# Attention in a two-block network: the value products of both heads of a pair share one bank of the small pool

## The chip, the cores and the metric

The kernel is one program on one core of a Trainium2 chip. The metric is the device time of one execution in microseconds (us), the median of three runs. The engines are named as in the profile: PE is TensorE (matmuls, and PEld its weight loads), DVE is VectorE, ACT is ScalarE, POOL is GpSimd, SP issues most of the DMAs.

## The reference, cut to what matters

Two small transformer networks run one after the other on 256 tokens of width 1024, everything in float32. The first has two layers: layer 0 with sparse and sliding-window attention (8 + 8 heads), layer 1 with dilated attention (16 heads). The second has two layers ("mixers") with two attention branches of 8 heads each, called fox and mla, beside a recurrent branch. All attention has this form per head, with 256 queries and 256 keys and a causal mask of one kind or another:

```
s  = einsum('qd,kd->qk', q, k) * scale          # scores
s  = where(mask, s, -inf)
p  = exp(s - max(s))
o  = einsum('qk,kd->qd', p, v) / sum(p)         # value products
...
def mixer layer:                                # second network
    z = rmsnorm(x) @ w_in                       # q, k, v of both branches, gates, recurrence
    y_b = attention of mla (z) @ w_br_b
    y_c = attention of fox (z) @ w_br_c
    merged = sigmoid(gates) * (y_a, y_b, y_c), summed
    x = x + merged @ w_o
    x = x + feed-forward(x)
```

Head size is 64; in the kernel a key of a fox head has 66 numbers and one of an mla head 96.

## The kernel before

Tokens lie in two tiles of 128 rows. All weight matrices are streamed: SP loads a block (`raw_block`, L216), ACT rounds it to the high part `wh` (L236), DVE takes the low part `wl` (L237), and PE multiplies three times per block (`mm3`, L249 to L253). These are the "dense" products.

The helper `attend` (L349) computes the attention of a pair of heads, and it runs 36 times: 12 times in layer 0 (`nsa_pair`, `b_pair`), 8 times in layer 1 (`attention`), 8 times in each mixer (`branch`, L993: four fox pairs, then four mla pairs). The steps of a pair, each once per head:

- scores (L358 through the helper `mm`): PE writes the scores of the first 128 queries to columns 256 to 383 of a PSUM bank and those of the other 128 queries to columns 0 to 255;
- softmax (L366, L367): DVE adds the mask and takes the row's minimum of the negated sum into `m`, ACT takes the exponent; both work on tile `pr` in SBUF;
- transposes (L375): PE turns the three 128x128 blocks of `pr` back into the same PSUM bank;
- eviction to `pt`: DVE for the first head (L381), ACT for the second (L379), or DVE for both with a multiplier in layer 1 (L377);
- value products (L385 to L387, recorded under L358): three matmuls of 65 columns. Column 64 of `v` is one, so it yields the sum of the exponents. They go to columns 0 to 129 of the same bank that held scores and transposes;
- DVE takes the reciprocal of the sums (L404) and scales the products into the accumulator (L398 and its like).

PSUM has eight banks in three pools: `psd` 2 banks (dense products), `psb` 4 banks, `psm` 2 banks. Before, a pair takes two banks of `psb`, one per head, and holds them from the first score to the last read of its value products, so two pairs fit. `psm` serves other short uses; in the mixers these are the transposes of queries and keys (`heads_T`, L983: four transposes per head, L986 and L988, then one copy by ACT, L990).

No order is written out by hand. A list scheduler orders the instructions of each engine by their place in the program and by when their inputs, a free buffer and their engine would be there. Each tag of a pool has a fixed number of buffers (`BUFS`, `psd`, `psb`, `psm`); a tile whose tag has none free waits, and in both programs the tiles of `psm`, and those of `psb`, are first written in the order in which the program names them. On the chip each engine takes its instructions strictly in the order that the scheduler fixed.

Of the kernel before, what the change touches and what calls it, by code (L numbers as in the profile page):

```python
# [147 lines left out]
def model(ctx: ExitStack, tc: tile.TileContext, A, out, taps=None):  # L148
# [4 lines left out]
    wk = pool("wk")  # L153
    sm = pool("sm", 12)
    ps = pool("ps", 1, space=bass.MemoryType.PSUM)
    BUFS = {"wr": 5, "wh": 5, "wl": 5, "xt": 16, "rg": 14, "acc": 2, "w512": 5, "qkT": 4, "pr": 2, "pt": 2, "vv": 8, "fa": 4, "qk": 2, "junk": 1, "cm": 1, "w128": 4}

    def tmp(shape, tag, name, dt=F32):
        return wk.tile([P] + list(shape), dt, name=name, tag=tag, bufs=BUFS[tag])

# [5 lines left out]
    def psb():  # L166
        return ps.tile([P, 512], F32, name="psb", tag="psb", bufs=4)

    def psm():
        return ps.tile([P, 512], F32, name="psm", tag="psm", bufs=2)  # L170
# [7 lines left out]
    def queue_after(ins, earlier):  # L178

        info = mybir.DependencyInfo(mybir.DependencyClass.NoSync, mybir.DependencyReason.DATA)  # L180
        for e in earlier:
            tc.add_manual_dep(ins.ins, e.ins.name, info, reason="function table")
        return ins
# [165 lines left out]
    def attend(q, k, v, mask, ct=False, sink=None):  # L349
# [4 lines left out]
        pr, pt = tmp([2, 384], "pr", "pr"), tmp([2, 384], "pt", "pt")  # L354
        two = lambda x: x.rearrange("p (a t) -> p a t", a=2)

        bank = [psb(), psb()]
        mm = lambda o, l, r, a, b: nc.tensor.matmul(o, l, r, start=a, stop=b, skip_group_check=True)  # L358
# [14 lines left out]
        for j in range(2):  # L373
# [5 lines left out]
                nc.scalar.activation(pt[:, j], bank[j][:, :384], AF.Copy)  # L379
            else:  # L380
                nc.vector.tensor_copy(pt[:, j], bank[j][:, :384])  # L381
        pov = []
        for j in range(2):
            o = bank[j][:, :130].rearrange("p (q e) -> p q e", q=2)
            mm(o[:, 0], pt[:, j, 256:], v(0, j), True, True)  # L385
            for kt in range(2):
                mm(o[:, 1], pt[:, j, kt * P:(kt + 1) * P], v(kt, j), False, kt == 1)  # L387
            pov.append(o)
# [148 lines left out]
    first = [win_e.load(*win_e.by[0][0])]  # L537
# [14 lines left out]
    def layer0(nm, after):  # L552
# [55 lines left out]
        for t in range(2):  # L608
            o = psd()
# [7 lines left out]
            z, e = small(24, "gz"), small(24, "ge")  # L617
# [7 lines left out]
        for t in range(2):  # L625
            o = psb()
# [142 lines left out]
        def attend_cmp(vbd):  # L769

            p = psm()
# [5 lines left out]
            th = lambda x: x.rearrange("p (t h) -> p t h", t=2)  # L777
            bc = lambda x: th(x)[:, :, :, None].to_broadcast([P, 2, 8, 16])
            per_t = lambda n: con(n)[:, :, None].to_broadcast([P, 2, 8])
            s = tmp([256], "cm", "cs")  # L780
            nc.vector.tensor_tensor(c4(s), c4(p[:, :256]), con("cmpm").rearrange("p (t c) -> p t c", t=2)[:, :, None, :].to_broadcast([P, 2, 8, 16]), op=ALU.add)
            m, dn, rc = (small(16, n_) for n_ in ("cm", "cd", "crc"))
            nc.vector.tensor_reduce(th(m), c4(s), axis=AX.X, op=ALU.max)
# [571 lines left out]
```

## Time and profile before

| | |
|---|---|
| median of three runs | 1586.75 us (1581.74 to 1588.69) |
| the profiled execution: its time | 1581.74 us |
| the profiled execution: its span, first to last instruction | 1580.0 us |
| PE busy | 1557.5 us, 99% of the span |
| DVE busy / ACT busy | 982.3 us (62%) / 855.3 us (54%) |
| TensorE clock granted, mean | 0.998 |

Stages in the span: layer 0 attention lies from about 38 to 122 us, layer 1 attention from 343 to 440 us, the attention of the first mixer from 690 to 742 us and that of the second from 1155 to 1207 us. Between them are dense products.

A PE that is busy is not always at its peak, since a matmul's end is modelled: two matmuls in a row overlap. So what PE does is read here by the distance of starts (the chain of waits lists those), and what it lacks by the idle part of a window.

### The profile page before, as it was taken

The numbers are of one execution on the slowest core, as the hardware profiler recorded it, in microseconds if no ns is written. First come the engines' busy times: TensorE is split into PE (matmuls) and PEld (weight loads), VectorE is DVE, ScalarE is ACT, GpSimd is POOL, SyncE is SP. The second block draws the span as 40 slices with busy tenths as digits, with TensorE's granted clock in tenths as the row PEclk, the third lists the DMA queues.
The fourth block names the chain that finished last, engine by engine and source line by source line (L and its number), as shares of the span: only waits on it lengthen the run. The fifth ranks groups of instructions, "written<-read, shape, count | busy, mean of one in ns | idle before, by whom it ended". The sixth has DMA issues, their size and how long they took to land.

```text
span 1580.0 us, 21686 instructions
## 1 busy us (share of the span) xinstructions
PE 1557.5 (99%) x7870; PEld 1314.7 (83%) x7870; DVE 982.3 (62%) x1778; ACT 855.3 (54%) x1385; POOL 140.3 (9%) x226
## 2 busy tenths in 40 slices
PE   8999999999999999999999999999999999999997
PEld 7778888899888888899888888888898888888886
DVE  6685545577765455576677655456575777655556
ACT  6555444455454444676474654446685564644445
POOL 2000000011100000120033000000020023000001
PEclk9999999999999999999999999999999999999999
DMA  7424655544545565451657555554552656465661
GB/s 270 149 92 133 206 184 184 187 141 131 182 131 191 186 192 188 161 180 40 196 179 233 174 181 192 186 188 160 177 169 71 204 189 197 161 201 185 197 195 61
DMA packets 80587, 269.53 MB, mean 171 GB/s; under 512 B 11360, under 2 KB 12768, under 8 KB 80480
## 3 DMA queue, kind: packets, MB, share of 16 engines
q1 hardware_dynamic: 80048, 267.10, 52.7%
q8 instruction: 62, 1.02, 0.3%
q10 hardware_dynamic: 432, 1.05, 0.2%
q14 instruction: 45, 0.37, 0.1%
HBM read 267.06 MB, written 1.05 MB: 170 GB/s over the span
## 4 chain that ended last, share of the span: by engine, by line
PE 96%; DVE 2%; ACT 1%; DMA 1%; issue 0%; POOL 0%; POOLq 0%; SPq 0%; DVEq 0%; ACTq 0%
PE psb L250 13%; PE psb L252 13%; PE psb L251 13%; PE psd L252 12%; PE psd L250 12%; PE psd L251 12%; PE psb L358 5%; PE psm L250 3%; PE psm L251 3%; PE psm L252 3%; PE psb L375 1%; PE psb L497 1%; DVE wl L237 1%; PE psb L270 1%; PE psm L270 1%; DMA wr<-w_in_e 1%
## 5 line engine op out<-in xcount | busy, mean ns | idle before, releaser
L237 DVE TENSOR_TENSOR wl<-wr,wh 128x1024 fp32r<-128x1024 f32 (+2 forms) x504 | 598.1, 1198 | 423.0 <-ACT wh L236 410.5
L236 ACT ACTIVATE wh<-wr 128x1024 fp32r<-128x1024 f32 (+2 forms) x504 | 512.6, 1029 | 474.0 <-PE psb L252 208.5
L251 PE MATMUL psb<-wl,th 128*128 128x512 f32 x912 | 349.4, 391 | 0.0
L252 PE MATMUL psb<-wh,tl 128*128 128x512 f32 x912 | 349.2, 390 | 0.0
L250 PE MATMUL psb<-wh,th 128*128 128x512 f32 x912 | 346.5, 391 | 0.0
L252 PE MATMUL psd<-wh,tl 128*128 128x512 f32 (+4 forms) x696 | 255.7, 370 | 3.4 <-DVE tl L279 3.4
L250 PE MATMUL psd<-wh,th 128*128 128x512 f32 (+4 forms) x696 | 258.2, 375 | 0.0
L251 PE MATMUL psd<-wl,th 128*128 128x512 f32 (+4 forms) x696 | 255.0, 369 | 0.5 <-DVE wl L237 0.5
L252 PEld LDWEIGHTS psb<-wh,tl 128*128 128x128 f32 x912 | 171.2, 188 | 35.7
L250 PEld LDWEIGHTS psb<-wh,th 128*128 128x128 f32 x912 | 171.3, 188 | 35.3
L251 PEld LDWEIGHTS psb<-wl,th 128*128 128x128 f32 x912 | 171.3, 188 | 35.2
L252 PEld LDWEIGHTS psd<-wh,tl 128*128 128x128 f32 x696 | 131.2, 188 | 22.7 <-DVE tl L279 5.0
L251 PEld LDWEIGHTS psd<-wl,th 128*128 128x128 f32 x696 | 131.5, 189 | 17.5 <-DVE wl L237 0.9
L250 PEld LDWEIGHTS psd<-wh,th 128*128 128x128 f32 x696 | 131.3, 189 | 17.5 <-issue 1.7
L306 POOL TENSOR_SCALAR rest<-ss 128x1 f32<-128x1 f32 x24 | 7.2, 299 | 919.4 <-ACT junk L316 919.4
L367 ACT ACTIVATE pr<-pr,m 128x128 f32<-128x128 f32 (+1 forms) x144 | 58.3, 447 | 29.9 <-DVE m L366 28.1
L250 PE MATMUL psd<-wh,hth 128*128 128x512 f32 x176 | 71.9, 412 | 0.0
L251 PE MATMUL psd<-wl,hth 128*128 128x512 f32 x176 | 68.8, 391 | 0.0
L251 PE MATMUL psm<-wl,hth 128*128 128x512 f32 x176 | 68.5, 389 | 0.0
L250 PE MATMUL psm<-wh,hth 128*128 128x512 f32 x176 | 68.5, 389 | 0.0
L252 PE MATMUL psm<-wh,htl 128*128 128x512 f32 x176 | 67.8, 389 | 0.0
L487 ACT ACTIVATE sg<-psb,r 128x256 f32<-128x256 f32 x88 | 41.8, 475 | 48.0 <-PE psb L252 47.8
(320 smaller groups left out, 1759.9 us busy)
## 6 DMA issues: line engine op xcount, KB each, us to landing
wr<-w_gate_up SPq DMA_DIRECT2D x176, 512.0 KB, 4.3
wr<-w_down SPq DMA_DIRECT2D x88, 512.0 KB, 3.3
wr<-w_in SPq DMA_DIRECT2D x88, 512.0 KB, 4.0
wr<-w_qkv_o SPq DMA_DIRECT2D x32, 384.0 KB, 3.5
wr<-w_o SPq DMA_DIRECT2D x16, 512.0 KB, 4.1
wr<-w_ple_gate SPq DMA_DIRECT2D x16, 512.0 KB, 4.0
wr<-w_in_e SPq DMA_DIRECT2D x10, 512.0 KB, 4.7
wr<-w_out_e SPq DMA_DIRECT2D x8, 512.0 KB, 4.6
```

The costliest lines, as they stand in the source:

```text
L236: nc.scalar.activation(hi[:, :m * n], raw, AF.Copy)
L237: nc.vector.tensor_tensor(lo[:, :m * n], raw, hi[:, :m * n].bitcast(F32), op=ALU.subtract)
L250: first = nc.tensor.matmul(o, xh, wh, start=start, stop=False)
L251: nc.tensor.matmul(o, xh, wl, start=False, stop=False)
L252: nc.tensor.matmul(o, xl, wh, start=False, stop=stop)
L270: turns.append(nc.tensor.transpose(p[:, j * P:(j + 1) * P], src[:, j * P:(j + 1) * P], ident))
L306: nc.gpsimd.tensor_scalar(rest, ms, self.eps, None, op0=ALU.add)
L358: mm = lambda o, l, r, a, b: nc.tensor.matmul(o, l, r, start=a, stop=b, skip_group_check=True)
L367: exps.append(nc.scalar.activation(e, e, AF.Exp, bias=neg, scale=-1.0))
L375: nc.tensor.transpose(bank[j][:, b * P:(b + 1) * P], pr[:, j, b * P:(b + 1) * P], ident)
L487: nc.scalar.activation(sg, o[:, :256], AF.Silu, scale=r)
L497: nc.tensor.transpose(pt[:, j * 256 + t * P:j * 256 + (t + 1) * P], hs[t][:, j * P:(j + 1) * P], ident)
```

## The change

`attend` takes one bank of `psm` for the value products of both heads (columns 0 to 129 for the first, 130 to 259 for the second) and no longer writes them over the two `psb` banks. Only the first matmul into that bank carries the start flag, so the second head's first matmul is ordered after it. The two `psb` banks of a pair are then free again after the evictions to `pt`. Tile `pr` gets a third buffer. The scratch `cs` of `attend_cmp` moves from a tag of its own to tag `qk`, and the tag `cm` goes.

```diff
-    BUFS = {... "pr": 2, "pt": 2, ... "junk": 1, "cm": 1, "w128": 4}
+    BUFS = {... "pr": 3, "pt": 2, ... "junk": 1, "w128": 4}
...
-        pov = []
+        both, pov = psm(), []
         for j in range(2):
-            o = bank[j][:, :130].rearrange("p (q e) -> p q e", q=2)
-            mm(o[:, 0], pt[:, j, 256:], v(0, j), True, True)
+            o = both[:, 130 * j:130 * j + 130].rearrange("p (q e) -> p q e", q=2)
+            i = mm(o[:, 0], pt[:, j, 256:], v(0, j), j == 0, True)
+            if j:
+                queue_after(i, [first])
+            else:
+                first = i
             for kt in range(2):
                 mm(o[:, 1], pt[:, j, kt * P:(kt + 1) * P], v(kt, j), False, kt == 1)
             pov.append(o)
...
-            s = tmp([256], "cm", "cs")
+            s = tmp([256], "qk", "cs")
```

PE has the same 7444 matmuls as before; the scheduler places those of the attention stages anew, and nearly all others as before. Lines behind the edit are numbered four higher in the changed kernel (`heads_T` at L990 and L992 there, L404 becomes L408, L398 becomes L402).

PE in a mixer, before: here fox pairs end and mla pairs begin. `psb<-vf,pt` are value products, `psb<-qkT` scores, `psb<-S,pr` transposes of `pr`, `psm<-S,...` the transposes of queries and keys of later heads.

```order
L358 MATMUL psb<-vf,pt 128x65 x3
L358 MATMUL psb<-qkT 128x128
L358 MATMUL psb<-qkT 128x256
L358 MATMUL psb<-qkT 128x128
L358 MATMUL psb<-qkT 128x256
L986 MATMUL psm<-S,qtok 96x128 x2
L988 MATMUL psm<-S,ktok 96x128 x2
L358 MATMUL psb<-qkT 128x128
L358 MATMUL psb<-qkT 128x256
L986 MATMUL psm<-S,qtok 96x128 x2
L988 MATMUL psm<-S,ktok 96x128 x2
L375 MATMUL psb<-S,pr 128x128 x6
```

PE in a mixer, now: from the first head's value products of one pair (A, the third fox pair) to the transposes of `pr` of the next pair's first head (B, the fourth). In the rows the heads follow as A first, B first, B first, A second, B second, B second, B first, A second, B second, B first.

```order
L358 MATMUL psm<-vf,pt 128x65 x3
L990 MATMUL psm<-S,fq 66x128 x2
L992 MATMUL psm<-S,fk 66x128 x2
L375 MATMUL psb<-S,pr 128x128 x3
L990 MATMUL psm<-S,fq 66x128 x2
L992 MATMUL psm<-S,fk 66x128 x2
L358 MATMUL psb<-qkT 128x128
L358 MATMUL psb<-qkT 128x256
L358 MATMUL psm<-vf,pt 128x65 x3
L358 MATMUL psb<-qkT 128x128
L358 MATMUL psb<-qkT 128x256
L375 MATMUL psb<-S,pr 128x128 x3
```

Before, the query and key transposes stood up to two pairs ahead of the scores they feed, and scores of two pairs stood together. Now B's query transposes follow A's first value products, and this pattern of 12 rows repeats from pair to pair with no dense product between them: from the second fox pair's scores to the last mla pair's scores, in both mixers.

DVE in a mixer, before, in the middle of the fox pairs. `ISA pr,m` is the masked minimum of L366 and `ISA m` the short instruction behind it that stores its result.

```order
L381 COPY pt_6563<-psb_6564 128x384
L1031 TENSOR_SCALAR vm_6755<-psd_6837,rk_6318 128x4x64
L366 ISA pr_6612,m_6611<-psb_6615,BM_69 128x128
L366 ISA m_6611 128x1
L366 ISA pr_6612,m_6611<-psb_6615,BM_69 128x256
L366 ISA m_6611 128x1
L1031 TENSOR_SCALAR vm_6756<-psd_6847,rk_6368 128x4x64
L237 TENSOR_TENSOR wl_7155<-wr_7152,wh_7154 128x1024
L404 RECIPROCAL rc_6592<-psb_6564 128x2
L381 COPY pt_6613<-psb_6614 128x384
L398 TENSOR_TENSOR acc_6546<-psb_6564,rc_6592 128x2x64
```

DVE in a mixer, now, over the same A (`psm_6708`) and B (`psb_6737`, `psb_6738`) as above:

```order
L366 ISA pr_6735,m_6734<-psb_6737,BM_69 128x128
L366 ISA m_6734 128x1
L366 ISA pr_6735,m_6734<-psb_6737,BM_69 128x256
L366 ISA m_6734 128x1
L408 RECIPROCAL rc_6715<-psm_6708 128x2
L408 RECIPROCAL rc_6715<-psm_6708 128x2
L402 TENSOR_TENSOR acc_6566<-psm_6708,rc_6715 128x2x64 x2
L366 ISA pr_6735,m_6734<-psb_6738,BM_69 128x128
L366 ISA m_6734 128x1
L366 ISA pr_6735,m_6734<-psb_6738,BM_69 128x256
L366 ISA m_6734 128x1
L381 COPY pt_6736<-psb_6737 128x384
```

The reads of A's value products now stand between the two heads of B, and the eviction of B's first head (the last row) behind B's second head; before, each head's reciprocal stood by itself.

PE at the end of layer 1, now, the seventh of eight pairs (`L897` are the query and key transposes of the eighth):

```order
L358 MATMUL psb<-qkT 128x128 x2
L358 MATMUL psb<-qkT 128x256 x2
L375 MATMUL psb<-S,pr 128x128 x6
L358 MATMUL psm<-v1,pt 128x65 x3
L897 MATMUL psm<-S,qk 128x128 x4
L358 MATMUL psm<-v1,pt 128x65 x3
```

Before, the scores of the seventh and the eighth pair stood together there, with twelve dense products around them; now the transposes of `pr` follow the pair's own scores with nothing between.

## Rows read from the trace of the kernel before

**Rows 1.** The page, busy time by engine: us, share of the span, instructions.

```profile
PE 1557.5 (99%) x7870; PEld 1314.7 (83%) x7870; DVE 982.3 (62%) x1778; ACT 855.3 (54%) x1385; POOL 140.3 (9%) x226
```

**Rows 2.** Windows: stretch, length, busy PE, PEld, DVE, ACT, POOL, clock, DMA.

```profile
38.00:122.00 84.00, 80.10 (x597) 65.94 (x596) 62.85 (x249) 43.24 (x103) 8.59 (x13) 1.00 0.34 114
343.00:440.00 97.00, 96.79 (x604) 87.19 (x603) 71.78 (x195) 47.17 (x89) 15.31 (x20) 1.00 0.47 147
...
690.00:742.00 52.00, 52.00 (x377) 48.28 (x376) 36.78 (x143) 38.38 (x84) 6.29 (x16) 1.00 0.35 112
...
1155.00:1207.00 52.00, 52.00 (x377) 48.28 (x376) 36.79 (x143) 38.35 (x84) 6.20 (x16) 1.00 0.36 112
```

**Rows 3.** Chain of waits, first mixer: start, us, engine and line (PE with PEld).

```profile
697.86 0.66 PE psb L358 x4
698.51 0.22 PE psm L986 x2
698.74 0.22 PE psm L988 x2
...
703.60 0.33 PE psb L375 x3
...
707.18 0.62 PE psb L358 x6
```

**Rows 4.** Chain of waits at the end of layer 1: one head, scores to products.

```profile
433.77 0.29 DVE pr L366
...
434.07 0.34 DVE pr L366
...
434.41 0.48 DVE pt L377
434.89 0.04 issue
```

**Rows 5.** Groups by line and shape, 694 to 742 us: count | busy us, mean ns.

```profile
L367 ACT ACTIVATE pr<-pr,m 128x256 f32<-128x256 f32 x16 | 8.0, 500 | 0.0
...
L237 DVE TENSOR_TENSOR wl<-wr,wh 128x1024 fp32r<-128x1024 f32 x5 | 6.1, 1218 | 0.8 <-ACT wh L236 0.8
...
L358 PE MATMUL psb<-qkT 96*128 96x256 f32 x16 | 4.8, 380 | 0.0
...
L990 ACT ACTIVATE qkT<-psm 96x512 f32<-96x512 f32 x8 | 4.6, 586 | 1.5 <-PE psb L358 1.5
...
L381 DVE COPY pt<-psb 128x384 f32<-128x384 f32 x8 | 4.4, 553 | 1.2 <-PE psb L375 1.0
...
L398 DVE TENSOR_TENSOR acc<-psb,rc 128x128 f32<-128x128 f32 x15 | 4.2, 288 | 0.3
...
L988 PE MATMUL psm<-S,ktok 128*96 128x128 f32 x16 | 3.0, 272 | 0.0
...
L404 DVE RECIPROCAL rc<-psb 128x2 f32<-128x2 f32 x16 | 2.6, 166 | 6.2 <-PE psb L358 5.9
```

**Rows 6.** Lines of layer 1: duration ns min/median/max, first and last start.

```profile
L896 DVE COPY qkT<-psm x8: 397/413/425, 349.3 to 424.4; 128x256 f32<-128x256 f32 x8
```

**Rows 7.** Lines of `compress` in layer 0, same columns.

```profile
L664 DVE TENSOR_REDUCE cu<-psm x2: 414/418/422, 59.6 to 75.3; 128x64 f32<-128x256 f32 x2
L666 ACT ACTIVATE ce<-cu x2: 242/243/244, 60.2 to 78.0; 128x64 f32<-128x64 f32 x2
L668 DVE RECIPROCAL ce<-ce x2: 531/538/546, 60.7 to 80.3; 128x64 f32<-128x64 f32 x2
```

**Rows 8.** Windows, columns as in Rows 2: the least busy PE, and the end.

```profile
96.00:106.00 10.00, 8.27 (x67) 6.72 (x66) 9.42 (x44) 4.79 (x14) 0.00 (x0) 1.00 0.18 54
...
1570.00:1580.00 10.00, 1.26 (x11) 1.06 (x9) 3.84 (x9) 3.19 (x8) 2.51 (x5) 0.67 0.28 106
```

More of the change, by code (lines that the diff above doesn't have):

```diff
@@ L155, in model @@
     ps = pool("ps", 1, space=bass.MemoryType.PSUM)
-    BUFS = {"wr": 5, "wh": 5, "wl": 5, "xt": 16, "rg": 14, "acc": 2, "w512": 5, "qkT": 4, "pr": 2, "pt": 2, "vv": 8, "fa": 4, "qk": 2, "junk": 1, "cm": 1, "w128": 4}
+    BUFS = {"wr": 5, "wh": 5, "wl": 5, "xt": 16, "rg": 14, "acc": 2, "w512": 5, "qkT": 4, "pr": 3, "pt": 2, "vv": 8, "fa": 4, "qk": 2, "junk": 1, "w128": 4}
     def tmp(shape, tag, name, dt=F32):
```

## The prediction

> **What bounds the kernel now.** I read the busy times first, then windows by stage, then the chain of waits inside the stages that the change touches. PE is busy for 1557.5 us of a span of 1580.0 us [rows 1], so everything that lengthens the run has to be idle time of PE, and everything that shortens it has to come out of 22.5 us of idle time, most of which lies at the start and at the end. In the attention of both mixers PE is busy for all of 52.00 us [rows 2], and in layer 1 it lacks 97.00 - 96.79 = 0.21 us. Only layer 0 has something to give: 84.00 - 80.10 = 3.90 us [rows 2]. So the change can win 4.1 us at most in its own stages, and it can lose much, if the order that it forces on PE no longer hides the softmax.
>
> The price list for one head in a mixer, as distances between starts: scores 0.66 us, four transposes of queries and keys 0.22 + 0.22 = 0.44, three transposes of `pr` 0.33, value products 0.62 [rows 3]; 2.05 per head, 4.10 per pair. What follows on other engines: masked minimum of a head 0.29 + 0.34 = 0.63 [rows 4], exponent of its larger part 0.50, copy of queries and keys 0.586, eviction to `pt` 0.553, a reciprocal 0.166, a scaling 0.288 [rows 5]. The hand-over from one engine to the next shows as 0.04 [rows 4]. A result comes later than the next matmul could start: the last transpose lasts 0.272 us where its followers start 0.11 apart, and the last score 0.380 at a distance of 0.22 [rows 3, 5]; I take 0.16 for both.
>
> **What the change does to the mixers.** It removes no instruction. It takes the value products out of `psb`, where four banks held two pairs at once, and puts them into `psm` with its two banks, in line with the transposes of queries and keys. Tiles of `psm` are written in program order, so the query transposes of pair B can't be placed before the value products of pair A are, and these come at the end of A's softmax. The order of PE shows this as fixed: value products of A's first head, then B's queries and keys. Before, those transposes ran up to two pairs ahead and filled every wait. Gate products could fill the waits, but their `psb` tile comes after that of the last pair in the program, and the order puts them there.
>
> So a pair now costs a chain. I start the clock at A's first value products.
> - 0.62 for these and 0.44 for B's first transposes: 1.06. The copy starts at 1.06 + 0.16 + 0.04 = 1.26 and ends at 1.85; B's second transposes start at 1.89. PE has A's transposes of `pr` for 0.33 of this: **0.50 idle**.
> - Transposes to 2.33, scores of B's first head to 2.99, result 3.15. DVE 3.19 to 3.82, exponent 3.86 to 4.36, transposes of `pr` from 4.40. PE has A's second value products and B's second scores, 0.62 + 0.66, until 4.27: **0.13 idle**.
> - Transposes to 4.73, result 4.89. DVE could evict from 4.93. But in its order stand two reciprocals (0.33) and two scalings (0.58) of A, from 3.82 to 4.73, then the minimum of B's second head, to 5.36, and only then the eviction, to 5.91. The next value products start at 5.95: **1.22 idle**; with a free DVE it would be 5.52 and 0.79.
>
> The period is thus 5.52 to 5.95 us against 4.10 of PE's work, 1.42 to 1.85 idle. I take 1.7, nearer the upper end, because the DVE order is in the program; small DVE operations overlap by a little. The order has five such periods from the second fox pair to the third mla pair: 8.5 us. Ahead of them the second fox pair goes through its softmax alone: copy 0.16 + 0.04 + 0.59 + 0.04 less scores 0.66 is 0.17; transposes of `pr` wait 0.16 + 0.04 + 0.63 + 0.04 + 0.50 + 0.04 = 1.41 less the second head's 0.83: 0.58; the eviction 0.79; together 1.5. A weight split of 1.218 us [rows 5] stands between its two heads on DVE, so up to 2.8. Behind them the last pair's second transposes wait 0.50 once more, and then gate products follow. **Per mixer 8.5 + 1.5 + 0.5 = 10.5 us**, from 9.0 (five at 1.42) to 14 (five at 1.85, the 2.8, and 0.11, the distance of one transpose, for each of some 15 restarts of PE). Before it was nothing there [rows 2], so two mixers cost **21 us, from 18 to 28**.
>
> **Layer 1.** Its transposes of queries and keys are under the same rule, but most pairs have twenty and more dense products between scores and transposes of `pr`, which hide 1.41 us easily. What stays: a hand-over from transposes to scores takes 0.16 + 0.04 + 0.41 [rows 6] + 0.04 = 0.65. At five of the pairs value products of 0.62 stand in it, at one nothing: 0.8 in sum. The last two pairs have no dense product between scores and `pr`: 0.16 + 0.04 + 0.34 + 0.04 + 0.50 + 0.04 less the last score's 0.22 is 0.90 for the first head, 0.50 - 0.33 = 0.17 for the second, 0.16 + 0.04 + 0.48 + 0.04 - 0.33 = 0.39 for the eviction, 1.5 us; in the eighth pair six other transposes take 0.66 of it off. 0.8 + 1.5 + 0.9 = 3.2, less the 0.21 of before: **3 us, from 0 to 5**.
>
> **Layer 0.** Here the order is turned about more than elsewhere: seven pairs with hardly a dense product first, then the dense products of two weight chunks, then the four sliding-window pairs. The third `pr` buffer lets scores run further ahead, and 3.90 us of idle PE [rows 2] may go. On the other side the small chain of `compress` for the keys, which had transposes and value products beside it, stands alone: 0.42 + 0.24 + 0.54 [rows 7] and hand-overs, some 1.4 us; and the first pair's softmax is as bare as before. I can't sum it closer: **+1 us, from -4 to +5**.
>
> The move of `cs`, the start flag on the first head alone and the removed tag cost nothing that I can see; `cs` is one 256-column tile in layer 0. In the mixers the third `pr` buffer brings nothing, since the `psm` order keeps two pairs in flight.
>
> One rule speaks against the change in another way. In the order of DVE before, the reciprocals of the two heads stand apart, each behind its own products; now both stand behind the second head's. The Trainium skill, "PSUM — Partial Sum Buffer", section on bank collisions, gives the reason: no other engine may touch a bank while PE writes it, whatever the address. Were the two heads guarded apart, DVE could read A's first head early and the eviction would be free at 4.93, which is the lower end of the period; no run here shows that.
>
> **Sum.** 21 + 3 + 1 = 25 us on the profiled execution's 1581.74 us is 1606.7. That run is the fastest of the three, 5 us below their median of 1586.75; on the median the same sum gives 1612. I predict 1609. The bounds add to 18 + 0 - 4 = 14 and 28 + 5 + 5 = 38, so 1596 to 1625 over both bases.
>
> **Rivals.**
> - *A longer chain.* DVE also splits weights, 1.218 us each [rows 5], and one of those in each period would add its length to the chain. The order shows one in the first period only. If hand-overs with several semaphores take 0.15 instead of 0.04, eight of them add 0.9 to a period: 10 periods and the ends give some 12 us more. 1621 to 1632.
> - *Not slower.* The score banks come free at the evictions, layer 0 gives back its 3.90 us and layer 1 its 0.21, and the mixers lose nothing because the chain of a pair is no longer than PE's 4.10 us of work: 1581.7 - 4.1 = 1577.6. It decides at a period of 4.10. Against it: the wait for the copy (0.50) and that for the eviction (0.79) have nothing beside them in PE's order, whatever the sizes elsewhere.
> - *The clock falls.* With 1.3 us idle in one piece and PE at 70% for some 30 us, the granted clock might go to its lower level of 1.2 GHz, half the speed. The part of the period that is PE's (0.62 + 0.44 + 0.44 + 0.66 + 0.33 = 2.49) would double: 12 times 2.5 is 30 us, 1639. Against it: at 8.27 busy of 10 us in layer 0 the clock stayed at 1.00, and it fell to 0.67 only where PE was busy for 1.26 of 10 us [rows 8]. The Trainium skill, "TensorE: Matmul & The Clock Gate", section on psum-queue depth-cycling, tells of a kernel whose micro-idles between groups of matmuls made the clock oscillate; the trace agrees that it falls in idleness, and has no stretch at 70%.
> - *The change doesn't do this:* the scheduler's order is in the program, so that much is certain; only the sizes are open.
>
> **How the numbers follow.** Forecast as worked out (1596 to 1621) 0.72, longer chain 0.14, clock 0.05, not slower or within noise 0.07, something else 0.02. For 8 in 10 the range takes the forecast and most of the longer chain: 1595 to 1628. Half a per cent, 7.9 us, is about what a measurement of this kernel can tell from no change. Faster by more would need twice the idle time of all attention stages: 0.02. Same 0.07, slower 0.91.
>
> **What would show it.** In the changed trace: PE idle of 9 to 14 us in each mixer's attention, at three places in each period (before transposes of keys and queries, waiting for ACT's copy; before transposes of `pr`, waiting for the exponent; before value products, waiting for DVE's eviction), at a distance of 5.5 to 6 us from pair to pair; the clock at 1.00 there; some 3 us idle at the end of layer 1; layer 0 about as long as before. A mixer's PE without idle, or a period under 5 us, would make the prediction wrong, and a layer 0 that changes by more than 5 us would make its sum wrong.

## The result and the profile after

The changed kernel takes 1657.89 us (median of 6 executions, 1651.27 to 1663.32) against 1587.3 us for the kernel before (6 executions, 1581.74 to 1588.69). The ratio over the executions is 1.0456, 95% interval 1.0425 to 1.0487 (the two medians alone give 1.0445). It is slower, as predicted, but by 71 us and not by 25. The profiled execution took 1651.27 us; its span is 1649.5 us, 69.5 us more than before. It is the fastest of the six and has the highest mean clock, 0.981; the three slowest, 1661.63 to 1663.32 us, have 0.968 to 0.972. So the lower clock takes more of the median's 71 us than of the 69.5 us that are read here.

I divide both traces at the same matmuls: layer 0 from its first scores to the first transposes of its feed-forward part (L497, now L501), and each later stage from the end of one feed-forward part (152.04 us long in every trace here) to the next. Microseconds:

| stage | before | after | difference | predicted |
|---|---|---|---|---|
| layer 0 | 120.8 | 144.3 | +23.5 | +1 (-4 to +5) |
| layer 1 | 160.4 | 168.2 | +7.8 | +3 (0 to 5) |
| first mixer | 289.3 | 305.0 | +15.7 | +10.5 (9 to 14) |
| second mixer | 312.9 | 335.1 | +22.1 | +10.5 (9 to 14) |

The start and the end of the program account for the remaining 0.4 us. The page of the kernel after, with busy time by engine and then the digits of PE and of its clock in 40 slices:

```profile
PE 1588.6 (96%) x7870; PEld 1333.2 (81%) x7870; DVE 979.7 (59%) x1778; ACT 863.3 (52%) x1385; POOL 136.5 (8%) x226
...
PE   8979999999899999998999999999988999999997
...
PEclk9979999999999999999999999999988999999999
```

PE executes 7870 instructions, as in [rows 1], but is busy 31.1 us longer with them. Busy time can grow in two ways: at a lower clock, and because a matmul ahead of a wait shows its whole modelled end, which the next matmul covers otherwise. The clock digits show the first, in layer 0 and in the second mixer; the second shows in run e13_claim below, where a stage at a clock of 1.00 is busy for 4.1 us longer. The other 38.4 us are idle time of PE. Windows of the changed kernel, columns as in [rows 2] (layer 0, layer 1, the first mixer ahead of and during its attention, the second mixer):

```profile
38.00:142.00 104.00, 89.83 (x585) 73.19 (x584) 63.35 (x252) 43.44 (x102) 7.61 (x13) 0.87 0.27 92
361.00:470.00 109.00, 98.66 (x633) 90.73 (x631) 72.95 (x200) 50.41 (x90) 14.78 (x22) 1.00 0.45 143
690.00:727.00 37.00, 37.00 (x206) 33.25 (x205) 22.02 (x54) 24.97 (x46) 8.02 (x20) 1.00 0.55 180
727.00:794.00 67.00, 58.06 (x360) 49.00 (x359) 31.92 (x126) 37.40 (x73) 3.70 (x12) 0.95 0.22 64
1207.00:1281.00 74.00, 65.38 (x366) 55.45 (x363) 32.66 (x128) 38.06 (x74) 4.29 (x14) 0.84 0.20 61
```

Both attentions of the mixers were without idle time before; now each has about 9 us (67.00 - 58.06 = 8.94; 74.00 - 65.38 = 8.62). The clock column is a mean over two levels, so the time at the lower level, 1.2 GHz, is twice the missing share: 2 x 0.05 x 67 = 6.7 us in the first mixer and 2 x 0.16 x 74 = 23.7 us in the second. The two mixers run the same code, and the second lost 22.1 - 15.7 = 6.4 us more with 17.0 us more at half clock: 0.38 us for each microsecond at half clock, and 13.2 us per mixer for the rest. It is less than the half that a PE busy all the time would lose, in part because slow work falls where PE would have waited.

The idle time of layer 1 grew by 10.34 - 0.21 = 10.1 us, but the stage by 7.8 us at a clock of 1.00. So idle time and time lost differ by some us, in either direction: in another order the same matmuls also start at other distances.

One period of a mixer, from the chain of waits of the kernel after (start, us, engine, tile and line; L990 and L992 are the transposes of queries and keys, L994 their copy):

```profile
760.37 0.88 PE psm L358 x6
761.25 0.22 PE psm L990 x2
761.47 0.23 PE psm L992 x2
...
761.79 0.60 ACT qkT L994
...
762.43 0.42 PE psm L990 x2
762.86 0.22 PE psm L992 x2
763.07 0.67 PE psb L358 x4
...
763.77 0.29 DVE pr L366
...
764.07 0.34 DVE pr L366
...
764.41 0.21 DVE rc L408 x2
764.62 0.46 DVE acc L402 x2
...
765.10 0.29 DVE pr L366
...
765.39 0.23 DVE pr L366
...
765.74 0.49 DVE pt L381
...
766.28 0.88 PE psm L358 x6
```

This is the chain that the prediction worked out, link by link: value products, the next pair's transposes, ACT's copy, the second transposes, scores, DVE's minimum, its reciprocals and scalings, the second minimum, the eviction to `pt`, value products again. From 760.37 to 766.28 it takes 5.91 us, and so do the periods behind it. The sizes of the links differ from the prediction's, though. PE's waits between 690 and 800 us (what it waited for, us in total, times, longest):

```profile
PE psm L358 <- DVE pt L381: 4.3, 6, 0.7
PE psm L990 <- ACT qkT L994: 2.1, 5, 0.4
```

In the period shown PE waits twice, 0.41 us for ACT's copy and 0.72 us for DVE's eviction, and is busy for 4.78 us; the prediction had 4.10 us of work and three waits of 0.50, 0.13 and 0.79 to 1.22 us. PE's links are longer (0.88 us for the first value products, where 0.62 stood) and DVE's shorter (0.67 us for reciprocals and scalings, where 0.91 stood). That the total agrees so well is partly luck, since these differences cancel.

Layer 0, PE's waits between 38 and 142 us (line, what it waited for, us in total, times, longest). L752 and L768 are the last products of the two `compress` chains, for keys and for values:

```profile
PE psm L768 <- DVE hvx L764: 5.3, 1, 5.3
PE psm L752 <- DVE ch L673: 1.9, 1, 1.9
```

And what the clock did there and in the first mixer, in windows of 5 us:

```profile
70.00:75.00 5.00, 3.04 (x31) 2.22 (x24) 2.08 (x8) 0.64 (x2) 0.00 (x0) 1.00 0.90 335
75.00:80.00 5.00, 5.00 (x28) 4.23 (x28) 2.77 (x11) 1.71 (x3) 0.00 (x0) 0.59 0.16 61
80.00:85.00 5.00, 5.00 (x24) 5.00 (x23) 3.59 (x20) 2.39 (x5) 0.00 (x0) 0.50 0.28 79
...
105.00:110.00 5.00, 2.73 (x23) 2.53 (x22) 3.34 (x5) 3.03 (x4) 0.00 (x0) 1.00 1.00 393
110.00:115.00 5.00, 1.93 (x9) 1.93 (x10) 4.12 (x11) 1.11 (x2) 0.00 (x0) 0.50 0.86 257
...
740.00:745.00 5.00, 3.43 (x24) 2.63 (x23) 4.14 (x16) 3.70 (x6) 0.90 (x2) 0.99 0.67 206
745.00:750.00 5.00, 4.18 (x18) 3.23 (x19) 1.48 (x6) 1.83 (x4) 0.00 (x0) 0.50 0.45 156
```

Each time the clock falls behind or within a stretch in which PE stood: the 1.9 us of the keys' chain lie in 70 to 75 us, the 5.3 us of the values' chain run from 107.8 to 113.1 us. In all, layer 0 has 2 x 0.13 x 104 = 27 us at half clock. But idle time in such a window does not decide by itself. The kernel before has one in layer 0 that was busy for less than the 3.43 us above, and its clock stayed at 1.00:

```profile
100.00:105.00 5.00, 3.27 (x21) 1.99 (x20) 4.78 (x28) 3.29 (x9) 0.00 (x0) 1.00 0.01 5
```

### The profile page after: what moved, and what is told of

Same layout as the page of the kernel before. It is cut to its first block, busy times and chain, and to the rows that moved or that the text cites. A ratio compares the mean times of both kernels' runs of the same rounds, so it can differ in the third digit from the quotient of the medians.

```text
span 1649.5 us, 21635 instructions
## 1 busy us (share of the span) xinstructions
PE 1588.6 (96%) x7870; PEld 1333.2 (81%) x7870; DVE 979.7 (59%) x1778; ACT 863.3 (52%) x1385; POOL 136.5 (8%) x226
## 4 chain that ended last, share of the span: by engine, by line
PE 86%; DVE 4%; ACT 2%; issue 1%; POOL 0%; POOLq 0%; ACTq 0%; DVEq 0%
PE psb L252 12%; PE psb L250 12%; PE psb L251 12%; PE psd L250 11%; PE psd L252 11%; PE psd L251 10%; PE psm L250 3%; PE psm L251 3%; PE psm L252 3%; PE psm L358 2%; PE psb L358 1%; PE psb L501 1%; DVE wl L237 1%; DVE pr L366 1%; PE psm L990 1%
## 5 line engine op out<-in xcount | busy, mean ns | idle before, releaser
L252 PE MATMUL psd<-wh,htl 128*128 128x512 f32 x176 | 67.5, 391 | 0.0
```

The source lines that it names most:

```text
L252: nc.tensor.matmul(o, xl, wh, start=False, stop=stop)
```

## The experiments

The theory to be tested: (a) tiles of the small pool `psm` are first written in program order, so that whatever follows value products in the program waits for them, and this alone makes the pairs serial; (b) the idle time drops the clock, which costs again; (c) in layer 0 the raw weights of `compress`, which hold four of five `wr` buffers, starve the weight stream. Rivals: the third `pr` buffer is at fault; sharing a bank is; the small pool has too few banks.

All stage times, in us (ratio over the executions to those of the kernel before, run beside it, with its 95% interval; stage times come from the profiled execution):

| run | layer 0 | layer 1 | mixer 1 | mixer 2 | ratio |
|---|---|---|---|---|---|
| kernel before | 120.8 | 160.4 | 289.3 | 312.9 | 1 |
| changed kernel | 144.3 | 168.2 | 305.0 | 335.1 | 1.0456 (1.0425 to 1.0487) |
| e1_layer0 | 145.1 | 160.5 | 289.4 | 313.1 | 1.0151 (1.0136 to 1.0166) |
| e2_layer1 | 125.9 | 169.3 | 289.4 | 312.9 | 1.0080 (1.0065 to 1.0095) |
| e3_mixers | 120.9 | 160.5 | 304.9 | 334.8 | 1.0258 (1.0231 to 1.0285) |
| e4_own | 125.8 | 160.5 | 289.4 | 313.0 | 1.0006 (0.9985 to 1.0027) |
| e5_bank0 | 130.7 | 160.6 | 289.4 | 313.0 | 1.0032 (1.0011 to 1.0053) |
| e6_early_cmp | 153.2 | 160.5 | 289.3 | 313.0 | 1.0133 (1.0113 to 1.0154) |
| e8_six_raw | 137.7 | 160.5 | 289.4 | 313.1 | 1.0093 (1.0075 to 1.0111) |
| e9_own_six_raw | 119.3 | 160.5 | 289.4 | 313.0 | 0.9979 (0.9966 to 0.9992) |
| e10_claim_cmp | 134.5 | 160.4 | 289.4 | 313.0 | 1.0045 (1.0030 to 1.0060) |
| e11_two_small | 129.4 | 160.5 | 318.9 | 339.4 | 1.0267 (1.0228 to 1.0307) |
| e12_three_small | 160.8 | 165.3 | 304.7 | 331.5 | 1.0450 (1.0435 to 1.0466) |
| e13_claim | 121.2 | 160.5 | 297.5 | 330.1 | 1.0124 (1.0098 to 1.0151) |
| e14_l1_claim | 120.9 | 160.6 | 289.4 | 313.0 | 1.0004 (0.9986 to 1.0022) |
| e15_l1_act | 128.0 | 170.4 | 289.4 | 312.9 | 1.0083 (1.0058 to 1.0109) |
| e16_best | 119.2 | 160.5 | 289.4 | 313.0 | 0.9976 (0.9963 to 0.9990) |

Beside e10 to e13 all seven executions of the kernel before took 1586.91 to 1590.34 us, where its medians beside the other runs are 1582.2 to 1583.79 us. So the ratios of these four come out 0.3 to 0.4% low, and their stage times say more.

**One stage at a time.** A flag chooses between the code of before and after; only the named stage passes it.

```diff
+        if not shared:
+            pov = []
+            for j in range(2):
+                o = bank[j][:, :130].rearrange("p (q e) -> p q e", q=2)
...
+            return pov, m
         both, pov = psm(), []
```

> The shared bank of the small pool only in layer 0 (both kinds of pairs there); in layer 1 and the mixers each head's products go to its own score bank again; third buffer for probabilities kept. Theory (each stage pays by itself, for its own queue in the small pool): the 23.5 us that layer 0 lost, so a time 20 to 25 us above the kernel before, the weight stream of layer 0 at one block per 5 us as in the changed kernel, and the two stretches at the lower clock in layer 0. Rival (the loss of layer 0 comes from the third buffer of probabilities, which lets scores run ahead of the weights): the same 20 to 25 us here, but also in the run that keeps only that buffer. Rival (the lower clock of a stage comes from something that lasts over stages): mixers also show stretches at half clock here; by the theory they show none.

> The shared bank only in layer 1, own banks elsewhere, third buffer kept. Theory: 6 to 9 us above the kernel before, all of it in layer 1 (7.8 us there in the changed kernel), the clock at 1.00. Rival (layer 1 was slowed by what layer 0 left behind, late loads or a lower clock): within 2 us of the kernel before.

> The shared bank only in the two mixers, own banks elsewhere, third buffer kept. Theory: a period of 5.9 us from pair to pair in the mixers, 9 to 10 us idle in each, plus stretches at half clock: 25 to 38 us above the kernel before, with the two mixers differing by as much as their stretches at half clock differ. Rival (the clock falls only because layer 0 was already idle): clock 1.00 in the mixers and 18 to 21 us above.

> Only the rest of the change: third buffer for probabilities, the compressed scores in the other tag; each head's products in its own score bank everywhere. Theory (the small pool's queue is all of it): within 4 us of the kernel before, and not above it by more than 2; a gain of up to 4 us if scores run further ahead in layer 0. Rival (third buffer at fault): 10 us or more above the kernel before, most of it in layer 0.

Measured: 1606.32, 1594.91, 1621.93 and 1584.62 us beside a kernel before of 1582.81: +23.5, +12.1, +39.1 and +1.8. The table shows that a stage that does not share is where it was, to 0.2 us in layer 1 and the mixers, and that the sharing stage has the loss of the changed kernel, to about 1 us (layer 1 of e2_layer1, expected at a clock of 1.00, has 3.4 us at half clock). So stages pay separately, and the third `pr` buffer and the tag of `cs` cost nothing that can be measured. Of the 12.1 us of the layer 1 run 5 us lie in layer 0, in code that is the same as in e3_mixers and e4_own; e4_own had them too. Windows of e4_own:

```profile
95.00:100.00 5.00, 4.08 (x38) 3.64 (x38) 4.52 (x22) 1.04 (x3) 0.00 (x0) 1.00 0.35 108
100.00:105.00 5.00, 4.51 (x24) 3.33 (x21) 4.33 (x23) 3.31 (x10) 0.00 (x0) 0.67 0.00 0
105.00:110.00 5.00, 5.00 (x21) 4.02 (x21) 1.12 (x7) 0.88 (x2) 0.00 (x0) 0.50 0.01 2
110.00:115.00 5.00, 5.00 (x13) 3.20 (x14) 2.30 (x13) 1.82 (x4) 0.00 (x0) 0.50 0.00 0
115.00:120.00 5.00, 5.00 (x40) 3.79 (x39) 3.85 (x15) 2.48 (x7) 0.00 (x0) 0.96 0.00 0
```

In that execution the clock fell behind a window that was 4.08 us busy; in e3_mixers, with the same layer 0, it did not, behind windows of 4.47 and 3.80 us, and layer 0 is 125.8 against 120.9 us. In e11_two_small below, once more with the same layer 0, it fell between 95 and 100 us, in a window busy for all of its 5.00 us and behind one of 4.51 us. So the same code loses its clock in some executions and keeps it in others, and a window's idle time does not tell which; what does, no run here shows. The two layers 0 also price a stretch at half clock with nothing else changed: 2 x 5 x (0.33 + 0.50 + 0.50 + 0.04) = 13.7 us at half clock cost 4.9 us, 0.36 for each.

The two mixers of e3_mixers, windows over their attention:

```profile
690.00:765.00 75.00, 66.06 (x404) 55.88 (x403) 39.31 (x145) 44.46 (x88) 5.16 (x15) 0.95 0.27 89
1172.00:1250.00 78.00, 70.43 (x388) 59.02 (x388) 37.12 (x141) 42.64 (x83) 5.17 (x15) 0.85 0.24 75
```

The clock falls in the mixers without a disturbed layer 0 ahead of them; the idle time of the stage itself is enough.

**Is it the sharing or the queue?** Three ways to hold the value products, in e5 for all stages, in the others for the mixers:

```diff
-        both, pov = psm(), []
+        both, pov = bank[0], []          # e5_bank0
```

```diff
-        both, pov = psm(), []
+        pov = []                         # e11_two_small
         for j in range(2):
-            o = both[:, 130 * j:130 * j + 130].rearrange("p (q e) -> p q e", q=2)
+            o = psm()[:, :130].rearrange("p (q e) -> p q e", q=2)
...
```

```diff
-tag="psb", bufs=4
+tag="psb", bufs=3                        # e12_three_small
-tag="psm", bufs=2
+tag="psm", bufs=3
```

> The value products of both heads share one bank, as in the changed kernel, but that bank is the first of the pair's own two score banks and not one of the small pool; all else as in the changed kernel. Theory (the small pool's queue is what costs, not the sharing): within 4 us of the run with own banks, so within 6 us of the kernel before; no idle PE in the mixers' attention and none of their transposes of queries and keys behind value products. Rival (sharing a bank costs, since one head's readers must wait for the other head's products): most of the 71 us, 1630 us or more.

> Mixers only: each head's value products in a tile of its own again, but both tiles from the small pool; nothing is shared. Theory (what costs is the place in the small pool's queue, whose tiles are first written in program order): as slow as the shared bank in the mixers, 1617 to 1632 us, the same period of 5.9 us or longer. Rival (what costs is that two heads share one bank): within 8 us of the kernel before.

> Mixers only, shared bank, with three banks in the small pool and three instead of four score banks. Theory (the order of first writes, not the number of banks): the next pair's transposes still come behind the value products, so 1615 to 1640 us and a period of 5.9 us or longer. Rival (two small banks are too few for transposes and products): the period goes to about 4.5 us and the time to 1585 to 1600 us.

Measured: 1591.92 us (before 1583.79), 1633.36 and 1660.38 us (before 1588.81). With both heads in one bank of `psb` the mixers are at 289.4 and 313.0 us and PE has no idle time in them; the window of e5_bank0 over the first one:

```profile
698.00:760.00 62.00, 62.00 (x424) 56.65 (x424) 40.78 (x153) 43.83 (x91) 8.05 (x19) 1.00 0.29 98
```

What is left of its 8.1 us, 2 us more than I had allowed, lies in layer 0, 130.7 us, at a stretch of half clock of the kind just shown. Sharing is not what costs. The counterpart, two banks but both from the small pool, is no better than the changed kernel. In the profiled execution both mixers are longer than there (318.9 and 339.4), partly because the clock falls for longer; but that execution, 1645.74 us, is the slowest of four (the others 1627.03 to 1639.09). Window of e11_two_small:

```profile
690.00:790.00 100.00, 94.83 (x463) 78.75 (x462) 50.02 (x172) 52.20 (x104) 10.48 (x28) 0.78 0.27 87
```

A third small bank leaves the mixers at 304.7 and 331.5 us against 304.9 and 334.8 with two: value products still begin 5.63 us apart, a little under the 5.9 that I expected, and the transposes still follow them in PE's order. So a further small bank changes nothing while the order stays; but this run also has one score bank less, and PE waits 0.62 us in each period for the exponent there, so it does not exclude the number of banks alone. Its total missed the expected 1615 to 1640 us because three score banks also cost layer 0 some 40 us and layer 1 some 5, which I had not counted.

**Taking the shared tile's turn early.** If the order of first writes is the cause, a first write that needs nothing should dissolve it. One transpose of 128 columns into columns of the bank that nobody reads:

```diff
         both, pov = psm(), []
+        extra = [nc.tensor.transpose(both[:, 384:512], ident, ident) for _ in range(1)]
...
                 first = i
+                queue_after(i, extra[-1:])
```

> Mixers only, shared bank, two small banks and four score banks as in the changed kernel; new is one extra transpose of 128 columns per pair into an unused part of the shared bank, which computes nothing but is the first write to that tile and may run as soon as the bank is free. Theory: the next pair's transposes may then run ahead of this pair's value products, the period falls from 5.9 to between 4.2 and 5 us, idle PE and the stretches at half clock in the mixers go, 1583 to 1600 us, although PE has 16 matmuls more to do. Rival (two banks are too few, or sharing costs): 1615 us or more.

> Shared bank in layer 1 only, with one extra transpose of 128 columns per pair as first write to the shared bank (computes nothing). Theory (layer 1 loses because the next pair's transposes of queries and keys come behind this pair's value products and then stand bare before their scores): half or more of the 8.9 us of layer 1 come back, layer 1 at 161 to 165 us against 169.3 with the shared bank and 160.5 with own banks. Rival (DVE's queue, which holds the copy of the keys back wherever the transposes are): 167 us or more.

Measured: 1608.91 us (before 1588.81) in the mixers, and 1583.39 us (before 1582.2) in layer 1. In layer 1 the whole loss is gone, 160.6 against 169.3 us; window of e14_l1_claim:

```profile
340.00:470.00 130.00, 127.54 (x767) 114.95 (x767) 90.80 (x228) 67.42 (x127) 17.37 (x28) 1.00 0.47 147
```

In the mixers less comes back; the total lies between the theory's and the rival's numbers. By the stages the mixers are 8.1 + 17.1 = 25.2 us above own banks, in place of 15.5 + 21.8 = 37.3 in e3_mixers: half of the loss is gone in the first, a fifth in the second, which has as much time at half clock as there. Windows of e13_claim over the two attentions:

```profile
690.00:755.00 65.00, 60.80 (x401) 52.74 (x400) 37.46 (x143) 42.20 (x86) 7.12 (x17) 1.00 0.28 90
1165.00:1240.00 75.00, 71.97 (x404) 62.43 (x403) 38.22 (x143) 43.22 (x87) 5.98 (x15) 0.84 0.27 86
```

Idle time in the first mixer is 4.2 us where e3_mixers has 8.9, and two pairs take 10.26 us there (731.67 to 741.93 us), 5.13 each, a little over the 4.2 to 5 us expected. Over the whole stage PE is also busy for 4.1 us longer than before, at a clock of 1.00; the eight extra transposes explain some 0.9 of it, the whole ends of matmuls ahead of waits probably much of the rest. While a shared tile holds one small bank, the transposes of two heads have the other one only and wait for ACT's copy; that the number of banks now matters, where it made no difference in e12, fits, but it was not tried with a third bank. These two rows also price the clock once more: same code, +8.1 us in the first mixer at 1.00, +17.1 in the second with 2 x 0.16 x 75 = 24 us at half clock, 0.38 us for each. The mixers of e11_two_small (2 x 0.22 x 100 = 44 us in the first, 34 in the second) give 0.30, those of e12_three_small (6.8 and 13.7 us) 0.47. So 0.38 is a middle value, and what follows from it is an estimate.

**Layer 0.** Three ways at its loss, all with the shared bank in layer 0 only. In e6 the calls `keys_cmp()` and `values_cmp()` stand earlier; in e8 there is one raw weight buffer more, with room taken from two other tags; in e10 the last products of each `compress` chain take their turn early.

```diff
-"wr": 5 ... "pr": 3 ... "w128": 4
+"wr": 6 ... "pr": 2 ... "w128": 2        # e8_six_raw
```

```diff
+            extra = [queue_after(nc.tensor.transpose(pk[:, 384:512], ident, ident), [last]) for _ in range(1)]   # e10_claim_cmp
...
+            extra = [queue_after(nc.tensor.transpose(pv[:, 384:512], ident, ident), [last]) for _ in range(1)]
...
```

> The shared bank in layer 0 only, as in the run of that name, but the two compress chains are written earlier in the program (the keys' ahead of the first pair, the values' right behind the second weight chunk), so that their small-pool tiles queue ahead of most pairs. Theory (layer 0 loses because compress comes late and its raw weights hold four of five buffers meanwhile): over half of the 23.5 us come back, 1583 to 1594 us. Rival (what costs in layer 0 are the pairs' own serial softmax chains, as in the mixers, wherever compress stands): 1602 us or more.

> The shared bank in layer 0 only, with six raw weight buffers in place of five (room taken from the third buffer of probabilities and two of four small key tiles). Theory (weights starve in layer 0 because four raw buffers wait for compress and one is left): with two left the issues of the weight stream come in pairs and a third to a half of the loss comes back, 1592 to 1600 us. Rival (buffers are not the limit; the bare compress chain and the pairs are): 1603 us or more, as with five.

> The shared bank in layer 0 only, and in each of the two compress chains one extra transpose of 128 columns into an unused part of the bank of its last products, placed right behind the chain's own transposes. It computes nothing; it is the first write to that tile, so that tiles behind it in the small pool (the pairs' value products) may be written while the chain is still in DVE and ACT. Theory (layer 0 loses because PE stands idle for 1.9 us and for 5 us in these two chains, and because each of these idle pieces is followed by 14 to 20 us at half clock): most of both goes, 1585 to 1596 us, with fewer or shorter stretches at half clock. Rival (the loss is the weight stream's, through the raw buffers that compress holds): they are held as long as before, 1602 us or more.

Measured: 1606.86 and 1599.75 us (before 1583.79), and 1596.32 us beside a kernel before that took 1588.81 us. I go by the stage, 153.2, 137.7 and 134.5 us against 145.1 in e1_layer0.

With the turn of its last products taken early, a chain has value products of the pairs beside it. Neither of its two waits is among PE's waits any more, and 2 x 0.03 x 122 = 7 us are left at half clock, where e1_layer0 has 2 x 0.11 x 152 = 33. Window of e10_claim_cmp over layer 0, and then the longest of its waits:

```profile
38.00:160.00 122.00, 111.33 (x718) 89.53 (x717) 80.55 (x279) 58.17 (x132) 9.37 (x16) 0.97 0.32 109
```

```profile
PE psd L250 <- DVE rb L432: 2.5, 1, 2.5
PE psb L375 <- ACT pr L367: 2.1, 3, 1.0
```

That is 10.6 of 24.3 us, less than the theory's "most": nearly all of it is the clock (26 us less at 0.38 make 10), while the idle time only went from 12.2 to 122 - 111.33 = 10.7 us. It moved from the chains, in two long pieces, to dense products that wait for DVE to free their bank and to others, in short ones. The two long waits were most of the clock's cause, then, and of the idle time only the place where it gathered.

Six raw buffers bring back a third, but not as I thought. The queue of the loads still waits as long for the first products of `compress`, PE's two long waits are still there (1.9 and 5.2 us), and idle time is 144 - 132.52 = 11.5 us over the stage against 152 - 139.84 = 12.2 in e1_layer0; what changed is the clock. Rows of e8_six_raw, first the wait of the load queue, then windows:

```profile
SPq L176 <- PE psm L669: 36.1, 2, 35.2
```

```profile
80.00:85.00 5.00, 5.00 (x32) 4.23 (x30) 3.61 (x11) 1.69 (x2) 0.00 (x0) 0.77 0.59 177
85.00:90.00 5.00, 5.00 (x38) 4.93 (x38) 4.17 (x20) 3.62 (x7) 0.00 (x0) 1.00 0.47 158
```

The clock is back within 80 to 85 us, where the changed kernel stayed at 0.50 (0.54 from 85 to 90 us); in the whole stage 17 us are at half clock, where e1_layer0 has 34. The same two waits were thus followed by half as much slow time, and what sets its length stays open. So (c) is true as a wait of the load queue; what a sixth buffer gives back, 7.4 us, comes by way of the clock, and the idle time stays. The earlier calls of e6 brought nothing (its stage also begins 7 us earlier, at 36.1 us, and ends 1 us later than in e1_layer0): the values' chain waited 1.9 us in place of 4.8, but dense products then waited 4.4 us for weight splits, since the weights of `compress` are loaded ahead of theirs, and the clock fell three times, for 38 us in all.

**Layer 1.** In the changed kernel PE waits in layer 1 like this:

```profile
PE psb L358 <- DVE qkT L900: 4.5, 5, 2.0
PE psd L250 <- ACT v L889: 2.6, 4, 0.9
PE psb L375 <- ACT pr L367: 1.7, 2, 1.3
```

Scores wait for DVE's copy of the keys. One run puts that copy on ACT:

```diff
-            nc.vector.tensor_copy(qk[:, 1], pq[:, 256:512])
+            nc.scalar.activation(qk[:, 1], pq[:, 256:512], AF.Copy)
```

> Shared bank in layer 1 only; the copy of the keys goes to ACT, behind the copy of the queries, in place of DVE. Theory (bare hand-over, in which DVE's queue makes up most of the 4.5 us that scores wait for this copy): 2 to 4 us of the 8.9 come back, layer 1 at 165 to 168 us; scores then wait for ACT, 0.3 to 0.6 us each time. Rival (the loss is in the waits of dense products and of the last pairs): 169 us, nothing comes back.

Measured: layer 1 at 170.4 us, nothing came back. The wait moved; PE's waits in layer 1 of e15_l1_act:

```profile
PE psd L250 <- ACT v L898: 4.1, 3, 1.9
...
PE psb L358 <- ACT qkT L909: 0.7, 1, 0.7
```

The wait for the copy fell from 4.5 to 0.7 us and that for ACT's values rose from 2.4 to 4.1. Idle time between 340 and 470 us did fall, from 10.6 us in e2_layer1 to 8.5, but 10 us were at half clock there, where e2_layer1 had 3.4, and that took it back. A wait's row names who came last, not what would help: only the order did, in e14_l1_claim.

**A version below both.** Own banks as before, with six raw buffers (room from `cm` and two of the `w128` tiles); the second label is the same program with more executions.

> Each head's products in its own bank everywhere, as in the kernel before, with six raw weight buffers (room from the third buffer of probabilities and two small key tiles). By the theory the kernel before loses little to raw buffers: layer 0 has 3.9 us of idle PE, and 5 us to 8 us more in those of its runs in which the clock drops there. 0 to 5 us below the kernel before; the rival (the stream is not limited by raw buffers at all) gives 0 within 2 us.

> Own score banks for the value products, six raw weight buffers, two buffers of probabilities: the same program as the earlier run with own banks and six raw buffers, here with more rounds. Theory: the kernel before has a stretch at half clock in layer 0 in some executions, which six raw buffers make rare: 2 to 8 us below the kernel before, more where the kernel before has that stretch in most executions; where it has none, 0.5 to 2 us. Rival: no difference beyond 1 us on any chip.

Measured: 1580.99 us (before 1583.79) and 1580.03 us (before 1582.2). The gain of 0.2% is small, but both intervals lie below 1. Of the 23 executions of the kernel before beside e16_best, 16 took 1580.2 to 1584.3 us at a mean clock of 0.996 to 0.998, and 7 took 1587.7 to 1589.7 us at 0.991 to 0.994; all 12 of e16_best took 1579.2 to 1582.0 us at 0.997 to 0.999, and of the 10 of e9_own_six_raw one took 1585.17 us at 0.995. So much of the gain is probably that the clock falls in fewer executions, in layer 0 as in e4_own; no trace here shows such an execution of the kernel before. Between the profiled executions, neither of which has it, layer 0 differs by 1.6 us.

## Why the prediction was right in sign and wrong in size

- **Mixers, the period: right, with some luck in its parts.** 5.52 to 5.95 us predicted, 5.91 measured, with DVE's order as the longer end had it: reciprocals and scalings (764.41 to 765.08) ahead of the second head's minimum. But PE waits 1.1 us of it and not 1.7, and its own part takes 4.78 us and not 4.10. Without the clock a mixer lost 13.2 us where I took 10.5 with an upper end of 14; the windows show 8.94 of it as idle time. Some 2 us more are probably the ends of the matmuls ahead of the 14 waits, 0.16 us each by the prediction's own figure, which count as busy; the rest I can't place.
- **The clock in the mixers: wrong.** "The clock at 1.00 there" was the forecast; at 0.38 us for each of 6.7 and 23.7 us it cost 2.5 and 8.9 us. I gave this rival 0.05 because in [rows 8] a window at 8.27 of 10 us kept its clock. One window that held is no evidence for a chain of gaps: here it fell behind windows at 3.04, 2.73 and 3.43 of 5 us, and once, in e4_own, behind one at 4.08. Nor would a finer look at the kernel before have helped, since its window at 3.27 of 5 us kept its clock in the execution traced. The rival's own price of 30 us was too high: it doubled PE's whole part of every period, where the rows show two stretches and 0.38 a microsecond. The Trainium skill, "TensorE: Matmul & The Clock Gate", section on psum-queue depth-cycling, describes a clock that swings with micro-idles between groups of matmuls; these rows agree, since in the mixers it fell and no single gap was above 1.1 us.
- **Layer 0: the step that failed most.** +1 predicted, +23.5 measured. I priced the keys' chain at 1.4 us, and 1.9 came. I left out that the values' chain goes bare in the same way, 5.3 us, and I counted 3.90 us of idle time of before as a gain that might come; idle time grew to 104 - 89.83 = 14.2. Above all no price stood for the clock behind such a gap: 27 us at half clock, about 10 us by the rate of 0.38 (0.36 by e4_own against e3_mixers, in layer 0 itself). Idle 10.3 and clock 10 make 20 of the 23.5 us; the 3 us left are no more than that price is uncertain by (8 to 13 us at 0.30 to 0.47). And why PE waits some 7 to 10 us more in layer 0 wherever `compress` stands is only half settled: the runs show that the chains' own order set most of the clock, not what would give the idle time back.
- **Layer 1: mis-sized.** 3 us predicted, 7.8 measured. The term was the hand-over from transposes to scores, 0.65 us at most in my sum, for a free DVE; the five waits took 4.5 us, up to 2.0 each. Besides, I did not follow what the late scores do to the dense products behind them, 2.6 us in four waits for ACT's copy of the values.
- **The parts priced at nothing: right.** The third buffer of probabilities, the tag of `cs` and the start flag cost 1.8 us in e4_own, within its interval of no difference.
- **The rival "not slower"** fell by the period, as argued. Its point, a period of 4.10 us, is never reached. Whether DVE's readers would go earlier if each head had its own bank, no run shows, since both small banks of e11_two_small came with other changes of the order.

In sum: about 48 us by waits, where the prediction had 25, and about 22 us ((27 + 6.7 + 23.7) x 0.38) by a clock that it held at 1.00 (17 to 27 us at 0.30 to 0.47, and the waits accordingly).

## What to carry to other kernels

A pool whose tiles are first written in program order is a queue: before a late result is put into it, list what the program writes behind it there, and give the late result a tile elsewhere or a first write that needs nothing. Price idle time of PE twice, as the wait and as the stretch at half clock that may follow it, with a chance, since the same code kept its clock in other executions; and do so for chains of short gaps too (none in the mixers of the changed kernel was above 1.1 us), not only for the longest. Where a chain loses its cover, price all its copies in the program.

## What the runs showed of the hardware that I had not expected

- A wait of 1.9 us in a window that was otherwise full (3.04 of 5 us busy) was followed by 13.7 us at 1.2 GHz. At 0.38 a microsecond that costs more than twice what the gap did. The kernel before had 3.27 of 5 us in one window and kept its clock; e11_two_small lost it in a window that was full.
- A microsecond at half clock cost 0.36 to 0.38 us in three pairs of stretches with the same code, 0.30 and 0.47 in two more, not 0.5.
- The kernel before does it too: 7 of the 23 executions beside e16_best took about 6.5 us more, at a lower mean clock. The 5 us between the two bases of the prediction, 1581.74 and 1586.75 us, are of the same size, so which base to take was probably a question of the clock.
- Work that computes nothing made a kernel faster: eight transposes of 128 columns in layer 1 took 8.7 us off it, since they changed the order and not the amount.
